# Second input's four transfers issued together, and its row squares moved to the first attention half

## The chip, the cores and the metric

The kernel runs on one core of one Trainium2 chip. The metric is the device time of one execution in microseconds (us); less is better. A core has a matmul engine (TensorE, PE in the profile; PEld is its weight load), a vector engine (VectorE, DVE), a scalar engine (ScalarE, ACT), GpSimd (POOL) and an engine that here only issues transfers (SyncE, SP). Each engine works through its own instructions in the order in which the program gives them. Transfers between the chip's main memory (HBM) and on-chip memory (SBUF) run on 16 DMA engines.

## The reference

```python
for layer in range(DEPTH):                      # DEPTH = 1, x is (1, 256, 2048)
    h = rms_norm(x, ln_pre_g[layer])
    proj = jnp.einsum('bsd,de->bse', h, w_in[layer])
    rnn_x, rnn_gate, q, k, v, attn_gate, g_rnn, g_attn = split_columns(proj)
    hr = rg_lru(rnn_x, ...)                     # convolution, gates, linear recurrence over tokens
    y_rnn = jnp.einsum('bsc,cd->bsd', hr * jax.nn.silu(rnn_gate), w_rnn_out[layer])
    ...                                         # q, k rotated; 24 heads in 3 groups with their own dilation
    y_attn = jnp.einsum('bsc,cd->bsd', o * jax.nn.silu(attn_gate), w_attn_out[layer])
    merged = jax.nn.sigmoid(g_rnn) * y_rnn + jax.nn.sigmoid(g_attn) * y_attn
    y = jnp.einsum('bsd,de->bse', merged, w_o[layer])
    x = x + rms_norm(y, ln_post_g[layer])
```

`rms_norm` divides each token's row by the root of its mean square. The kernel multiplies by the gain before the projections and by the row's factor (`rstd`) after them.

## The kernel before

Every projection is made with float32 split in two: a high half (`wh`, `xh`) and a low half (`wl`, `xl`), and three matmuls (lines 283 to 285) in place of one: wh x xh, wl x xh, wh x xl. A projection of 512 columns has 16 rows of weight tiles. It goes in eight steps of a *pair* of them; with two token halves a pair is 12 matmuls. The weights come as transfers of 1 MB (`raw_...`, two pairs each, line 230) into three buffers, and each pair is split by ACT into `wh` (line 256) and by DVE into `wl` (line 257), into four buffers. `next_pair` keeps the splits some three pairs ahead of PE. The weight pairs of projection ga0 are called ga_0, ga_2, ... ga_14 here, by the first of their two tile rows.

The input is needed twice: for attention with its tokens in a turned order (`xh`, `xl`), and in their natural order for the gates and the recurrent branch. The second one comes in four transfers of 512 KB (`xnr0` to `xnr3`, line 179) and is split with the gain into `nh` by ACT (line 151) and `nl` by DVE (line 152), two instructions at a time. Its row factors `rstd_t` come from `row_stats` (lines 307 to 321): four transfers of rows (`xst`), four ACT squares that also add up, then a square root and a reciprocal.

The order of the program is: projections q, k (three groups), v (three groups) and the attention gate (`ag`) of half 0 of the heads, the same for half 1, then four gates `ga0` to `ga3` on the second x, and then the recurrent branch, its output and the last projection. Between the steps of a projection, `tick` lets other work proceed: the scores of a head, the shipping of its turned probabilities (`pt4` to `pt7` in half 1: 16 transfers of 32 KB each, line 84), their copy into `pr` (line 555), the weighted sums (`oo`, line 569). `load_in_time` is a generator that is advanced once per step of `ag1` and then of the gates (`along` in `proj_tok`). What it and the other jobs emit falls into the engines' queues at that place. SP's queue holds all transfers. A transfer into a tile waits until the last reader of the buffer's former tile is done; a raw buffer's last reader is the DVE split. Tiles of 512 KB share a pool of 29 buffers.

Of the kernel before, what the change touches and what calls it, by code (L numbers as in the profile page):

```python
# [42 lines left out]
def hybrid_block(ctx: ExitStack, tc: tile.TileContext, xc_rows, xct, xn_rows, xnt, par, g_post, w_in, w_rg, w_ig,  # L43
# [15 lines left out]
    def bigt(name, dt=F32):  # L59
        return big.tile([P, 1024], dt, name=name, tag="big", bufs=NBIG)  # L60
# [25 lines left out]
    def split_turned(t, name):  # L86

        h, l = bigt(f"{name}h", F32R), bigt(f"{name}l", F32R)
        src, h4, l4 = (a.rearrange(f"p ({o}) -> p u c i", u=8, c=4, i=32)
                       for a, o in ((t, "u c i"), (h, "c u i"), (l, "c u i")))  # L90
        nc.scalar.activation(h4, src, AF.Copy)
        nc.vector.tensor_tensor(l4, src, h4.bitcast(F32), op=ALU.subtract)
        return h, l
# [16 lines left out]
    def tick():  # L110
        now[0] += 1
        heavy = True
        for job in list(jobs):
            if job[0] <= now[0] and (heavy or job[2]):
                heavy = heavy and job[2]
                step(job)

    def step(job):
        try:
            d = next(job[1])  # L120
            job[2] = isinstance(d, float)
            job[0] = now[0] + int(d)
        except StopIteration:
            jobs.remove(job)

    def spawn(gen):
        job = [now[0], gen, False]
        jobs.append(job)
        step(job)
# [17 lines left out]
    def split_x(t, h, l, q, k):  # L147

        s = slice(k * S, (k + 1) * S)
        gk = par_sb[:, GP, q * 4 + k:q * 4 + k + 1]  # L150
        nc.scalar.activation(h[:, s], t[:, s], AF.Copy, scale=gk)
        nc.vector.scalar_tensor_tensor(l[:, s], t[:, s], gk, h[:, s].bitcast(F32), op0=ALU.mult, op1=ALU.subtract)
# [20 lines left out]

    def load_in_time():

        ts = [bigt(f"xnr{q}") for q in range(2)]

        def fetch(q):
            nc.sync.dma_start(ts[q].rearrange("p (k n) -> p k n", n=S),
                              xnt[q * 512:(q + 1) * 512, :].rearrange("(k p) n -> p k n", p=P))  # L180

        fetch(0)
        yield
        fetch(1)
        yield
        for q in range(4):
            h, l = bigt(f"nh{q}", F32R), bigt(f"nl{q}", F32R)
            if q >= 2:
                ts.append(bigt(f"xnr{q}"))
                fetch(q)  # L190
            for k in range(4):
                split_x(ts[q], h, l, q, k)
                nh.append(h[:, k * S:(k + 1) * S])
                nl.append(l[:, k * S:(k + 1) * S])
                if k % 2:
                    yield
# [73 lines left out]
    def next_pair(tag):  # L270
        while len(ready) <= AHEAD:
            p = next(stream, None)
            if p is None:
                break
            ready.append(p)
        p = ready.pop(0)
        assert p[0] == tag
        return p[1], p[2]

    def mm_tok(acc, t, k, lh, ll, wh, wl, nk):  # L280
        ts = slice(t * P, (t + 1) * P)
        acc = acc[t] if isinstance(acc, list) else acc[:, t, :]
        nc.tensor.matmul(acc, lh[k][:, ts], wh, start=(k == 0), stop=False)  # L283
        nc.tensor.matmul(acc, lh[k][:, ts], wl, start=False, stop=False)  # L284
        nc.tensor.matmul(acc, ll[k][:, ts], wh, start=False, stop=(k == nk - 1))  # L285

    def proj_tok(lh, ll, nk, tag, acc=None, steps=None, along=iter(())):

        if acc is None:
            acc = ps_acc.tile([P, 2, GRP], F32, name=f"acc_{tag}", tag="acc")  # L290
        for _ in range(steps or nk // 2):
            k0, pair = next_pair(tag)
            for kk, (wh, wl) in enumerate(pair):
                for t in range(2):
                    mm_tok(acc, t, k0 + kk, lh, ll, wh, wl, nk)
            next(along, None)
            tick()
        return acc
# [6 lines left out]
    rstd_t = const.tile([P, 2], F32, name="rstd_t")  # L305

    def row_stats(dst, rows, name):
        ss = const.tile([P, 2, 2], F32, name=f"ss{name}")
        xs = [[bigt(f"xs{name}{t}{i}") for i in range(2)] for t in range(2)]
        for t in range(2):  # L310
            for i in range(2):
                nc.sync.dma_start(xs[t][i], rows[t * P:(t + 1) * P, i * 1024:(i + 1) * 1024])
        yield 2
        for t in range(2):
            for i in range(2):
                nc.scalar.activation(xs[t][i], xs[t][i], AF.Square, accum_out=ss[:, t, i:i + 1])
                yield 1
        nc.vector.tensor_reduce(dst, ss, axis=AX.X, op=ALU.add)
        nc.vector.tensor_scalar(dst, dst, 1.0 / D, EPS, op0=ALU.mult, op1=ALU.add)
        nc.scalar.activation(dst, dst, AF.Sqrt)  # L320
        nc.vector.reciprocal(dst, dst)

    def norm_stats(kind, acc):
        yield from row_stats(rstd, xc_rows, "c")
        yield from qk_group(kind, 0, 0, acc)
# [138 lines left out]
    def qk_group(kind, g, half, acc):  # L464
        tr = bigt(f"{kind}T{g}{half}")
        hf = ROT // 2
        turned = Turn(tr, f"{kind}{g}{half}")
        for t in range(2):
            if t:
                yield 1  # L470
            r = work.tile([P, 4, 4, 32], F32, name=f"{kind}r{g}{half}{t}", tag="rope")
            nc.scalar.activation(r.rearrange("p e h j -> p h e j"), acc[:, t, :].rearrange("p (h e j) -> p h e j", h=4, e=4),
                                 AF.Copy, scale=rstd[:, t:t + 1])
            m = work.tile([P, 2, 4, ROT], F32, name=f"{kind}m{g}{half}{t}", tag="ropem")
            rot = r[:, 0]
            cosb = trig_sb[:, t, 0, :].unsqueeze(1).to_broadcast([P, 4, ROT])
            nc.vector.tensor_tensor(m[:, 0], rot, cosb, op=ALU.mult)
            for o in range(2):
                sn = trig_sb[:, t, 1, o * hf:(o + 1) * hf].unsqueeze(1).to_broadcast([P, 4, hf])
                nc.vector.tensor_tensor(m[:, 1, :, o * hf:(o + 1) * hf], rot[:, :, (1 - o) * hf:(2 - o) * hf], sn,  # L480
                                        op=ALU.mult)
            nc.vector.tensor_tensor(rot, m[:, 0], m[:, 1], op=ALU.add)
            turned.take(t, r.rearrange("p e h j -> p (e h j)"))
        yield from turned.ship()
        yield 5
        if g == 0:
            qkv[kind, g, half] = tuple(a.rearrange("p (c n) -> p c n", c=4) for a in split_turned(tr, f"{kind}s{half}"))
        elif kind == "q":
            q = bigt(f"qc{g}{half}")
            nc.scalar.activation(q.rearrange("p (h u i) -> p u h i", h=4, u=8), tr.rearrange("p (u h i) -> p u h i", u=8, h=4), AF.Copy)  # L490
            qkv[kind, g, half] = q.rearrange("p (h n) -> p h n", h=4)
        else:
            qkv[kind, g, half] = tr.rearrange("p (t b h i) -> p t b h i", t=2, b=4, h=4)
# [95 lines left out]
    def after(n, gen):  # L589
        yield n  # L590
        yield from gen


    for half in range(2):
        for g in range(NG):
            if half == 0 and g == 0:
                spawn(norm_stats("q", proj_tok(xh, xl, NK, "q00")))
                nc.sync.dma_start(trig_sb, trig)
                nc.sync.dma_start(mask_sb, masks)
                spawn(qk_group("k", g, half, proj_tok(xh, xl, NK, "k00")))  # L600
            else:
                spawn(qk_group("q", g, half, proj_tok(xh, xl, NK, f"q{g}{half}")))
                spawn(qk_group("k", g, half, proj_tok(xh, xl, NK, f"k{g}{half}")))
        for hh in range(4):
            spawn(after(3, scores(half, hh)))
        if half:
            spawn(row_stats(rstd_t, xn_rows, "t"))
        for g in range(NG):
            v_group(g, half, proj_tok(xh, xl, NK, f"v{g}{half}"))
        x2 = load_in_time() if half else iter(())  # L610
        attn_gate(half, proj_tok(xh, xl, NK, f"ag{half}", along=x2))
        for hh in range(4):
            spawn(after(2, weighted(half, hh)))
# [183 lines left out]
```

## Time and profile before

| what | value |
|---|---|
| median of 3 runs | 1080.38 us (1079.28 to 1081.52) |
| the profiled execution: its time | 1080.39 us |
| its span, from the first to the last instruction | 1078.6 us |
| PE busy | 1054.8 us (98%) |
| DVE busy | 652.9 us (61%) |
| ACT busy | 581.0 us (54%) |
| mean granted clock | 0.991 |

The busy shares are means over the span. PE is near 100% almost everywhere, and the page's row of 40 slices shows PE at 9 tenths or more in all but four of them: the first (8), the last (6), and two next to each other from 458 to 512 us (7 and 8), where the granted clock also falls to 8 tenths. "Granted clock" 1.00 is 2.4 GHz, 0.50 is 1.2 GHz. In a timeline the first number is the start in us from the span's start, the second the length, and the brackets give the idle time of the engine before it and what ended that. A matmul of PE is shown with 0.39 us, but one starts each 0.23 us, since they overlap.

### The profile page before, as it was taken

Reading aid. Unit: us, or ns where it says so; the run is one execution under the profiler, and the core shown is the slowest. Engines: PE = TensorE matmul, PEld = TensorE weight load, DVE = VectorE, ACT = ScalarE, POOL = GpSimd, SP = SyncE. Lnnn points to the kernel's source line nnn. Section 1 sums busy time; section 2 is a strip of 40 time slices with the busy share of each in tenths; the row PEclk is TensorE's granted clock in tenths of the full one; section 3 lists DMA queues with packets and bytes.
Section 4 is the critical chain, followed back from the end, with each engine's and each line's share of the span. In section 5 each row is a group of like instructions: output and inputs, shape, how many; then the busy total and the mean of one; then the engine's idle time right before and its main releaser. Section 6 shows DMA issues by size and latency. Waiting matters only on the chain.

```text
span 1078.6 us, 12939 instructions
## 1 busy us (share of the span) xinstructions
PE 1054.8 (98%) x4774; PEld 875.0 (81%) x4774; DVE 652.9 (61%) x831; ACT 581.0 (54%) x716; POOL 3.0 (0%) x7
## 2 busy tenths in 40 slices
PE   8999999999999999978999999999999999999996
PEld 7888888888888888857888888888888888888785
DVE  6666555646655646445654585876757746666455
ACT  7645445553544545463644457657767665444443
POOL 0000000000000000000000000000000000000000
PEclk9999999999999999988999999999999999999999
DMA  9868675565767774744666665666666655666872
GB/s 325 313 199 266 209 230 170 160 221 193 233 204 244 249 252 156 230 154 148 205 201 212 213 215 192 203 227 200 206 199 213 217 170 199 197 209 204 288 255 78
DMA packets 153263, 228.03 MB, mean 211 GB/s; under 512 B 12528, under 2 KB 56304, under 8 KB 153200
## 3 DMA queue, kind: packets, MB, share of 16 engines
q1 hardware_dynamic: 153200, 227.21, 64.9%
q8 instruction: 37, 0.61, 0.2%
q14 instruction: 26, 0.21, 0.1%
HBM read 207.23 MB, written 2.10 MB: 194 GB/s over the span
## 4 chain that ended last, share of the span: by engine, by line
PE 46%; DVE 3%; DMA 2%; ACT 1%; SPq 1%; issue 0%; ACTq 0%; DVEq 0%
PE acc_rx L283 3%; PE acc_rx L284 3%; PE acc_rx L285 3%; PE acc_rg L285 3%; PE acc_rg L283 3%; PE acc_rg L284 3%; PE acc_gr L284 3%; PE acc_gr L285 3%; PE acc_gr L283 3%; PE acc_ga L284 2%; PE acc_ga L285 2%; PE acc_ga L283 2%; PE acc_o L284 2%; PE acc_o L285 2%; PE acc_o L283 2%; PE acc_ro L284 2%
## 5 line engine op out<-in xcount | busy, mean ns | idle before, releaser
L257 DVE TENSOR_TENSOR wl_v<-raw_v,wh_v 128x1024 fp32r<-128x1024 f32 x48 | 58.2, 1216 | 56.5 <-ACT wh_v L256 56.5
L257 DVE TENSOR_TENSOR wl_k<-raw_k,wh_k 128x1024 fp32r<-128x1024 f32 x48 | 58.2, 1217 | 44.7 <-ACT wh_k L256 44.7
L256 ACT ACTIVATE wh_k<-raw_k 128x1024 fp32r<-128x1024 f32 x48 | 50.7, 1059 | 60.7 <-PE acc_q L285 26.6
L257 DVE TENSOR_TENSOR wl_q<-raw_q,wh_q 128x1024 fp32r<-128x1024 f32 (+1 forms) x50 | 58.6, 1173 | 38.3 <-ACT wh_q L256 36.5
L283 PE MATMUL acc_v<-wh_v,xh 128*128 128x512 f32 x192 | 76.3, 398 | 0.0
L283 PE MATMUL acc_q<-wh_q,xh 128*128 128x512 f32 x192 | 75.3, 392 | 1.0 <-ACT wh_q L256 1.0
L284 PE MATMUL acc_q<-wl_q,xh 128*128 128x512 f32 x192 | 74.9, 390 | 0.8 <-DVE wl_q L257 0.8
L285 PE MATMUL acc_v<-wh_v,xl 128*128 128x512 f32 x192 | 74.9, 390 | 0.0
L285 PE MATMUL acc_q<-wh_q,xl 128*128 128x512 f32 x192 | 74.9, 390 | 0.0
L284 PE MATMUL acc_v<-wl_v,xh 128*128 128x512 f32 x192 | 74.7, 389 | 0.0
L284 PE MATMUL acc_k<-wl_k,xh 128*128 128x512 f32 x192 | 74.7, 389 | 0.0
L283 PE MATMUL acc_k<-wh_k,xh 128*128 128x512 f32 x192 | 74.7, 389 | 0.0
L285 PE MATMUL acc_k<-wh_k,xl 128*128 128x512 f32 x192 | 74.7, 389 | 0.0
L256 ACT ACTIVATE wh_q<-raw_q 128x1024 fp32r<-128x1024 f32 (+1 forms) x50 | 51.0, 1025 | 42.7 <-PE acc_q L285 22.2
L256 ACT ACTIVATE wh_v<-raw_v 128x1024 fp32r<-128x1024 f32 x48 | 50.2, 1054 | 33.3 <-PE acc_v L285 23.4
L283 PE MATMUL acc_ga<-wh_ga,nh 128*128 128x512 f32 x128 | 52.0, 406 | 8.0 <-ACT wh_ga L256 8.0
L257 DVE TENSOR_TENSOR wl_rx<-raw_rx,wh_rx 128x1024 fp32r<-128x1024 f32 x32 | 39.1, 1223 | 34.0 <-ACT wh_rx L256 33.8
L257 DVE TENSOR_TENSOR wl_ga<-raw_ga,wh_ga 128x1024 fp32r<-128x1024 f32 x32 | 39.2, 1224 | 30.5 <-ACT wh_ga L256 30.4
L256 ACT ACTIVATE wh_ro<-raw_ro 128x1024 fp32r<-128x1024 f32 x32 | 33.5, 1058 | 38.3 <-PE acc_ro L285 33.6
L257 DVE TENSOR_TENSOR wl_rg<-raw_rg,wh_rg 128x1024 fp32r<-128x1024 f32 x32 | 38.8, 1220 | 25.4 <-ACT wh_rg L256 25.4
L284 PE MATMUL acc_ga<-wl_ga,nh 128*128 128x512 f32 x128 | 52.2, 408 | 1.7 <-DVE wl_ga L257 1.7
L257 DVE TENSOR_TENSOR wl_o<-raw_o,wh_o 128x1024 fp32r<-128x1024 f32 x32 | 38.3, 1220 | 24.2 <-ACT wh_o L256 24.2
(301 smaller groups left out, 2681.5 us busy)
## 6 DMA issues: line engine op xcount, KB each, us to landing
raw_k<-in_w_in_dram SPq DMA_DIRECT2D x24, 1024.0 KB, 5.4
raw_v<-in_w_in_dram SPq DMA_DIRECT2D x24, 1024.0 KB, 5.4
raw_q<-in_w_in_dram SPq DMA_DIRECT2D x20, 1024.0 KB, 5.7
raw_ga<-in_w_in_dram SPq DMA_DIRECT2D x16, 1024.0 KB, 5.2
raw_rx<-in_w_in_dram SPq DMA_DIRECT2D x16, 1024.0 KB, 5.5
raw_rg<-in_w_in_dram SPq DMA_DIRECT2D x16, 1024.0 KB, 5.1
raw_gr<-in_w_in_dram SPq DMA_DIRECT2D x16, 1024.0 KB, 5.5
raw_ro<-in_w_rnn_out_dram SPq DMA_DIRECT2D x16, 1024.0 KB, 5.4
```

The costliest lines, as they stand in the source:

```text
L256: nc.scalar.activation(h[:, i:i + m, :], src, AF.Copy)
L257: nc.vector.tensor_tensor(l[:, i:i + m, :], src, h[:, i:i + m, :].bitcast(F32), op=ALU.subtract)
L283: nc.tensor.matmul(acc, lh[k][:, ts], wh, start=(k == 0), stop=False)
L284: nc.tensor.matmul(acc, lh[k][:, ts], wl, start=False, stop=False)
L285: nc.tensor.matmul(acc, ll[k][:, ts], wh, start=False, stop=(k == nk - 1))
```

## The change

All four transfers of the second x are issued at two neighbouring steps of `ag1` (two and two), and the splits of its pairs begin one step later than before. `row_stats` for the second norm is started in half 0, after the projections of group 1, and no longer in half 1.

```diff
--- before.py
+++ after.py
@@ -173,21 +173,16 @@
 
     def load_in_time():
 
-        ts = [bigt(f"xnr{q}") for q in range(2)]
-
-        def fetch(q):
+        ts = []
+        for q in range(4):
+            ts.append(bigt(f"xnr{q}"))
             nc.sync.dma_start(ts[q].rearrange("p (k n) -> p k n", n=S),
                               xnt[q * 512:(q + 1) * 512, :].rearrange("(k p) n -> p k n", p=P))
-
-        fetch(0)
-        yield
-        fetch(1)
+            if q % 2:
+                yield
         yield
         for q in range(4):
             h, l = bigt(f"nh{q}", F32R), bigt(f"nl{q}", F32R)
-            if q >= 2:
-                ts.append(bigt(f"xnr{q}"))
-                fetch(q)
             for k in range(4):
                 split_x(ts[q], h, l, q, k)
                 nh.append(h[:, k * S:(k + 1) * S])
@@ -601,10 +596,10 @@
             else:
                 spawn(qk_group("q", g, half, proj_tok(xh, xl, NK, f"q{g}{half}")))
                 spawn(qk_group("k", g, half, proj_tok(xh, xl, NK, f"k{g}{half}")))
+            if half == 0 and g == 1:
+                spawn(row_stats(rstd_t, xn_rows, "t"))
         for hh in range(4):
             spawn(after(3, scores(half, hh)))
-        if half:
-            spawn(row_stats(rstd_t, xn_rows, "t"))
         for g in range(NG):
             v_group(g, half, proj_tok(xh, xl, NK, f"v{g}{half}"))
         x2 = load_in_time() if half else iter(())
```

The order in SP's queue at the end of half 1 was this (raw_ga0_0 is the first 1 MB of weights of ga0, pt7 the last head's turned probabilities, xnr0 to xnr3 the second x):

```order
L230 DMA raw_ga0_0_3704<-in_w_in_dram 128x4x512
L179 DMA xnr0_3718<-in_xnt_dram 128x4x256
L84 DMA pt7_3692<-trp7_3693 32x2x128 x4
L179 DMA xnr1_3719<-in_xnt_dram 128x4x256
L84 DMA pt7_3692<-trp7_3693 32x2x128 x4
L230 DMA raw_ga0_1_3754<-in_w_in_dram 128x4x512
L84 DMA pt7_3692<-trp7_3693 32x2x128 x8
L230 DMA raw_ga0_2_3808<-in_w_in_dram 128x4x512
L230 DMA raw_ga0_3_3857<-in_w_in_dram 128x4x512
L179 DMA xnr2_3873<-in_xnt_dram 128x4x256
L230 DMA raw_ga1_0_3914<-in_w_in_dram 128x4x512
L179 DMA xnr3_3930<-in_xnt_dram 128x4x256
```

It is now this:

```order
L225 DMA raw_ga0_0_3712<-in_w_in_dram 128x4x512
L179 DMA xnr0_3726<-in_xnt_dram 128x4x256
L179 DMA xnr1_3728<-in_xnt_dram 128x4x256
L84 DMA pt7_3700<-trp7_3701 32x2x128 x4
L179 DMA xnr2_3750<-in_xnt_dram 128x4x256
L179 DMA xnr3_3752<-in_xnt_dram 128x4x256
L84 DMA pt7_3700<-trp7_3701 32x2x128 x4
L225 DMA raw_ga0_1_3765<-in_w_in_dram 128x4x512
L84 DMA pt7_3700<-trp7_3701 32x2x128 x8
L225 DMA raw_ga0_2_3813<-in_w_in_dram 128x4x512
```

xnr2 and xnr3 moved from behind three weight transfers to between the pt7 transfers.

On ACT, from the split of pair ag1_12 to that of ga0_4, there stood (xst are the squares, nh the split of the second x, pr7 the copy of the last head's probabilities):

```order
L256 ACTIVATE wh_ag1_12_3779<-raw_ag1_3_3654 128x1024
L151 ACTIVATE nh0_3768<-xnr0_3718,par_sb_94 128x256 x2
L316 ACTIVATE xst10_3081,sst_3078<-xst10_3081 128x1024
L256 ACTIVATE wh_ag1_14_3804<-raw_ag1_3_3654 128x1024
L151 ACTIVATE nh1_3822<-xnr1_3719,par_sb_94 128x256 x2
L316 ACTIVATE xst11_3082,sst_3078<-xst11_3082 128x1024
L256 ACTIVATE wh_ga0_0_3829<-raw_ga0_0_3704 128x1024
...
L256 ACTIVATE wh_ga0_2_3853<-raw_ga0_0_3704 128x1024
L151 ACTIVATE nh2_3871<-xnr2_3873,par_sb_94 128x256 x2
L555 ACTIVATE pr7_3879<-pt7_3692 128x4x4x32 x2
L256 ACTIVATE wh_ga0_4_3882<-raw_ga0_1_3754 128x1024
```

There now stands:

```order
L251 ACTIVATE wh_ag1_12_3783<-raw_ag1_3_3662 128x1024
L151 ACTIVATE nh0_3799<-xnr0_3726,par_sb_94 128x256 x2
L251 ACTIVATE wh_ag1_14_3809<-raw_ag1_3_3662 128x1024
L151 ACTIVATE nh0_3799<-xnr0_3726,par_sb_94 128x256 x2
L251 ACTIVATE wh_ga0_0_3831<-raw_ga0_0_3712 128x1024
L151 ACTIVATE nh1_3847<-xnr1_3728,par_sb_94 128x256 x2
L251 ACTIVATE wh_ga0_2_3853<-raw_ga0_0_3712 128x1024
L151 ACTIVATE nh1_3847<-xnr1_3728,par_sb_94 128x256 x2
L550 ACTIVATE pr7_3875<-pt7_3700 128x4x4x32 x2
L251 ACTIVATE wh_ga0_4_3878<-raw_ga0_1_3765 128x1024
```

The squares and the square root are gone from here, and only nh0 and nh1, no longer nh2, stand ahead of pr7. In the first half the squares stand on ACT between the weight splits of group 2's q and k (q20, k20), and their transfers on SP behind the last q20 transfer:

```order
L225 DMA raw_q20_3_832<-in_w_in_dram 128x4x512
L307 DMA xst00_873<-in_xn_rows_dram 128x1024
L307 DMA xst01_874<-in_xn_rows_dram 128x1024
L307 DMA xst10_875<-in_xn_rows_dram 128x1024
L307 DMA xst11_876<-in_xn_rows_dram 128x1024
L225 DMA raw_k20_0_886<-in_w_in_dram 128x4x512
```

Before, the two weight transfers stood there next to each other. PE's order is the same in both kernels.

## Rows read from the trace of the kernel before

**Rows 1.** PE's waits between 430 and 530: total us, times, longest us.
```profile
PE acc_ga L283 <- ACT wh_ga L256: 8.0, 2, 4.9
PE acc_ga L284 <- DVE wl_ga L257: 1.7, 3, 0.8
```

**Rows 2.** Stretches: length, busy PE, PEld, DVE, ACT, POOL; PEclk, DMA share, GB/s.
```profile
460.00:465.00 5.00, 3.57 (x14) 2.66 (x15) 3.59 (x6) 5.00 (x9) 0.00 (x0) 1.00 0.79 256
...
480.00:485.00 5.00, 4.05 (x9) 2.87 (x10) 2.04 (x4) 4.98 (x9) 0.00 (x0) 0.50 0.00 0
```

**Rows 3.** Timeline of SP's DMA queue: start, length, what is issued.
```profile
450.22 0.53 SPq L230 DMA_DIRECT2D raw_ga<-in_w_in_dram  x1
...
450.85 0.51 SPq L179 DMA_DIRECT2D xnr<-in_xnt_dram  x1
...
451.42 3.17 SPq L84 DMA_DIRECT2D pt<-trp  x4
...
459.60 5.64 SPq L84 DMA_DIRECT2D pt<-trp  x8
...
471.41 0.50 SPq L179 DMA_DIRECT2D xnr<-in_xnt_dram  x1
...
487.79 0.50 SPq L179 DMA_DIRECT2D xnr<-in_xnt_dram  x1
```

**Rows 4.** Timeline of ACT; in brackets the idle time before, and its releaser.
```profile
457.71 0.91 ACT L151 ACTIVATE nh<-xnr,par_sb 128x256 fp32r<-128x256 f32 x2 [1.89 <-DMA xnr<-in_xnt_dram]
...
477.54 0.91 ACT L151 ACTIVATE nh<-xnr,par_sb 128x256 fp32r<-128x256 f32 x2 [7.84 <-DMA xnr<-in_xnt_dram]
...
478.35 1.13 ACT L555 ACTIVATE pr<-pt 128x512 f32<-128x512 f32 x2
```

**Rows 5.** Timeline of PE in the same stretch.
```profile
459.57 0.40 PE L285 MATMUL acc_ag<-wh_ag,xl 128*128 128x512 f32 x1
...
480.49 0.79 PE L283 MATMUL acc_ga<-wh_ga,nh 128*128 128x512 f32 x1 [4.86 <-ACT wh_ga L256]
...
481.75 0.79 PE L284 MATMUL acc_ga<-wl_ga,nh 128*128 128x512 f32 x1 [0.47 <-DVE wl_ga L257]
...
486.45 1.95 PE L569 MATMUL oo<-v,pr 128*128 128x128 f32 x16
...
488.16 0.48 PE L283 MATMUL acc_ga<-wh_ga,nh 128*128 128x512 f32 x1
...
491.00 1.95 PE L569 MATMUL oo<-v,pr 128*128 128x128 f32 x16
...
504.44 0.48 PE L283 MATMUL acc_ga<-wh_ga,nh 128*128 128x512 f32 x1
```

**Rows 6.** Timeline of DVE in the same stretch.
```profile
486.12 1.22 DVE L257 TENSOR_TENSOR wl_ga<-raw_ga,wh_ga 128x1024 fp32r<-128x1024 f32 x1
```

**Rows 7.** DMA issues from 450.7, then from 465.2: KB each, us to landing.
```profile
raw_ga<-in_w_in_dram SPq DMA_DIRECT2D x1, 1024.0 KB, 5.7
xnr<-in_xnt_dram SPq DMA_DIRECT2D x1, 512.0 KB, 6.8
...
pt<-trp SPq DMA_DIRECT2D x1, 32.0 KB, 2.3
```

**Rows 8.** A stretch near the kernel's start, columns as in rows 2.
```profile
10.00:15.00 5.00, 3.27 (x13) 2.11 (x12) 3.51 (x7) 3.87 (x8) 0.00 (x0) 1.00 1.06 381
```

**Rows 9.** First half: timelines of SP and ACT, then the tile xst.
```profile
93.67 0.54 SPq L230 DMA_DIRECT2D raw_q<-in_w_in_dram  x1
...
106.38 1.06 ACT L256 ACTIVATE wh_q<-raw_q 128x1024 fp32r<-128x1024 f32 x1 [1.66 <-PE acc_q L285]
...
L316 ACT ACTIVATE xst<-xst x4: 1041/1046/1051, 445.6 to 464.1; 128x1024 f32<-128x1024 f32 x4
L316 ACT ACTIVATION_READ_ACCUMULATOR xst<-xst x4: 185/186/193, 446.6 to 465.0; 128x1 f32 x4
...
DMA to landing us min/median/max: 6.6/7.7/8.7
```


## Prediction

> **What bounds the kernel now.** I read the page first: TensorE (PE) is busy for almost the whole span, so time can only be won where PE waits, where its clock is low, or at the two ends. The list of PE's waits around the second x shows that the waiting has one place: the first gate projection on the second x, acc_ga, waited 8.0 us in two waits for the high halves of its weights (wh_ga, made on ACT) and 1.7 us in three for the low halves (wl_ga, made on DVE) [rows 1]. The stretches of 5 us say the same from the other side: 3.57 us of 5 busy from 460, and from 480 to 485 the granted clock is 0.50, the lower of the two levels, 1.2 GHz [rows 2]. The reader is to see that the clock is still 1.00 where PE idles from 460, and low only behind a longer wait, that of 4.9.
>
> Why are wh_ga late? ACT runs in order, and just before those weights it stood for 1.89 us until xnr landed, and again for 7.84 us [rows 4]. xnr is the second x. The queue of SP explains it: its first transfer goes out at 450.85, but the third only at 471.41 and the fourth at 487.79 [rows 3]. They stand behind weight transfers (raw_ga) that wait for a buffer, and such a buffer comes free only when DVE has split older weights, which needs ACT. So ACT waits for xnr, xnr for SP, SP for a raw buffer, and the raw buffer for PE, ACT and DVE. The stall feeds itself twice.
>
> How much is it worth? PE's last undisturbed matmul before all this starts at 459.57, and pair ga_10 (the sixth of the eight weight pairs of ga0) begins at 504.44 [rows 5]. With a pitch of 0.23 the next matmul was due at 459.80, so the stretch is 44.64 us long. The work in it is four pairs of twelve matmuls at 2.72 (where PE sets the pace, ACT splits one pair in 1.06 and waits 1.66 for PE [rows 9]), four groups oo at 1.71 (486.45 to 488.16), and three pairs that follow an oo at 2.84 (488.16 to 491.00) [rows 5]: 10.88 + 6.84 + 8.52 = 26.2 us. The loss is 44.6 - 26.2 = **18.4 us**, waits and low clock together. That is the most that the change can give back here.
>
> **The change, part by part.** (1) The four xnr transfers are issued at two neighbouring steps, all ahead of the second raw_ga transfer. By SP's rhythm xnr0 and xnr1 go out at about 450.9 and 451.4, xnr2 and xnr3 after four pt transfers, at about 455.3 and 455.9. The buffers of xnr2 and xnr3 were last read by half 1's score phase (pt4 and qs1h), ahead of ag1 on their engines, so I see no new wait for a buffer. Both ACT waits for xnr go away.
>
> (2) The squares leave this stretch: four ACTIVATEs of about 1.05 us with a read of 0.19 each [rows 9], a square root with its table load, and three tiny DVE instructions. ACT then reaches the split of ag_14 earlier. Replayed by the rows: nh0 cannot start before xnr0 lands at 457.71 [rows 4], 0.91 for two nh, then the split of ag_14 by about 459.7 and its low half on DVE 1.2 later, 460.9. PE needs it at 459.80 + 2.72 = 462.5. So the waits before and in ag_12 go, and ga_0 starts at 465.2.
>
> (3) What is late next? ACT has split pair ga_2 and the nh behind it by about 464.5 (three nh couples and two splits from 459.7) and then stands before pr7 (the copy of the last head's turned probabilities), which waits for all sixteen pt7 transfers. Before, this copy started at 478.35, behind xnr2 [rows 4], and the wait was covered. Behind it on ACT stand wh_ga_4, nh2, the attention gate (agz, ags) with its table load, and wh_ga_6. PE will wait for those. So the time T at which pr7 starts decides the sum.
>
> T from rows: the last pt7 transfer was issued at 459.60 + 5.64 = 465.24 and landed 2.3 us later, at 467.5 [rows 3, 7]. Two more issues now stand ahead of it, 0.57 each (450.85 to 451.42): T is at least 467.5 + 1.1 = 468.6. From above: their bytes share the 16 DMA engines too. raw_ga, issued at 450.22, landed at 455.9 and xnr0, right behind it, at 450.85 + 6.8 = 457.65 [rows 3, 7], so 512 KB cost 1.73 us, two of them 3.5; if none of it fits into a gap, T = 468.6 + 3.5 = 472.1. I take the middle, **T = 470.3**, because the DMA engines still had some room then (0.79 busy from 460) [rows 2].
>
> The Trainium skill, page "DMA: Bandwidth & Descriptors", section Specifications, gives a core about 358 GB/s from HBM; by that 512 KB would be an estimated 1.46 us, the two 2.9, and T in the middle 470.0 in place of 470.3. No row shows that rate for an xnr alone; the sum keeps the row's 1.73.
>
> (4) From T on I carry over the distances of before, where the same ACT instructions stood in the same order behind pr7: wl_ga_4's matmul started at 481.75, which is 478.35 + 3.4; wl_ga_6 was split at 486.12 to 487.34, which is 9.0 behind 478.35 [rows 4 to 6]. PE comes to ga_4 at 465.2 + 2 x 2.72 + 1.71 = 472.4 and could take its low half at 472.7, but gets it at T + 3.4 = 473.7: a wait of 1.0. The rest of the pair takes 2.5, oo5 1.7; the low half of ga_6 comes at T + 9.0 = 479.3 where PE was ready at T + 7.9: 1.1 more. Then 2.5, oo6 1.7, ga_8 2.84 and oo7 1.71: ga_10 begins at T + 17.8 = 488.1. Before it was 504.44, so the gain is 486.7 - T, or **16.4 us**, with a cap of 18.4 (reached at T below 468.3). The bounds of T give 18.1 and 14.6.
>
> (5) Does the clock stay up? Two waits of about 1 us in some 7 us. At the start of the kernel PE was busy 3.27 us of 5, 1.7 idle, with the clock at 1.00 [rows 8]; it fell behind the wait of 4.9 [rows 1, 2]. The expected waits are close to the first, so I count no low clock.
>
> (6) What is added in the first half: four xst transfers of 512 KB right behind raw_q at 93.67, four squares and the square root. Landing took 6.6 to 8.7 us [rows 9], so they are there from about 101 to 105; the squares stand behind four splits, the third of which started at 106.38, one each 2.72. ACT's free time there is 1.66 us in each 2.72 [rows 9], and a square with its read is 1.24: it fits. I cost this part at nothing. Its cover is that ACT waits for PE, not PE for ACT; if a square waits for its transfer, ACT must be held for more than about two pairs of PE, 5 us (of four buffers for split weights at least two are full), before PE feels it, and without any cover the four cost 5.0 us. SP's next weight transfer waits for a raw buffer, one of which comes free every second pair, 5.4 us, so four issues at SP's pace of 0.6 ahead of it, 2.4 us, delay nothing. The square root no longer needs a table of its own where it now stands, between copies; the removed load lay in ACT time that had slack, so it is not counted.
>
> **Sum.** Profiled execution 1080.39 us (span 1078.6 and 1.8 around it; the median of the runs is 1080.38, the same), less 16.4: **1064.0 us**. Behind ga0 the page's slices show PE at nine tenths or more, so the rest should move as a block.
>
> **The rivals.** *Full cover*: pt7 isn't delayed by the extra transfers, or lands in gaps; T below 468.3, gain 18.4, 1062.0 us. For it: the last pt7 had landed at 467.5. Against: two issues and 1 MB stand in front of it. *The wait moves to pt7 and takes the clock with it*: transfers of pt7 queue behind xnr1 to xnr3 longer than their bytes say, because each issue on SP can also wait for an earlier one to land; T near 474.5, so PE waits 5 us at ga_4 and the clock falls once more. Gain 486.7 - 474.5 = 12.2, less the 2.2 that a pair took longer at the lower level (4.70 from 481.75 to 486.45 for what takes 2.5): 10.0, so 1070.4 us. For it: four pt issues behind xnr0 took 3.17 us, 0.8 each, those behind raw_ga 0.7 [rows 3], so SP does feel what is in flight. Against: only two of the four are new ahead of pt7. *Slower than before*: the xst transfers in the first half hold ACT, and through it the weights of k20. It decides from the point at which ACT stands for more than 5 + 16.4 = 21.4 us before a square; a landing of 31 us (a stand of 23) would cost about 2 us net, 1082. The longest landing seen was 8.7 us [rows 9]. *The change does nothing*: the tile buffers of xnr2 and xnr3 come free only with ga0, so their transfers wait where they are now and hold SP's queue: 1080. The order of last readers speaks against it.
>
> **How the numbers follow.** The likeliest case (T from 468.3 to 472.1) 0.72, full cover 0.10, the wait at pt7 with a lower clock 0.14, no effect 0.02, slower 0.02. A measurement of this kernel can tell about 0.2% (2 us) from no change. Faster: 0.72 + 0.10 + 0.14 = 0.96. The range: from 1061.5 (full cover, and half a microsecond of spread between runs) up to 1068.0, which is the likeliest case's upper end, 1080.4 - 14.6 = 1065.8, plus one short fall of the clock; it leaves out most of the pt7 rival and the last two, under 0.2.
>
> **What would show each step right or wrong.** Right: four xnr issues before 457, no ACT wait for xnr above 2 us after the first, a new ACT wait of about 6 us for pt in front of pr7, PE waits of acc_ga of 1 us or less each on wl_ga, granted clock 1.00 from 460 to 510, and ga_10 near 488. Step 3 is wrong if pr7 starts outside 468 to 472.5; step 5 if a stretch there shows a clock below 0.95; step 6 if PE shows a wait between 95 and 130 or ACT waits more than 2 us for xst. The sum is wrong if a wait that the long stall has hidden so far, for instance weights of ga1 behind the same queue, comes up after ga0.

## The result and the profile after

The changed kernel took 1065.12 us (median of 4 runs, 1064.78 to 1066.12), the kernel before 1080.52 in the same comparison (median of 4, 1079.28 to 1081.52): ratio 0.986, 95% interval 0.9843 to 0.9877. The prediction was 1064.0, with a range of 1061.5 to 1068.0. The profiled execution of the changed kernel took 1065.36 us (span 1063.6, mean granted clock 0.998 in place of 0.991).

First the queue of SP after the change, which answers to [rows 3]. (Lines 151 and 179 have stayed, those from 230 on are 5 less than before, 6 less in the kernels with the earlier fetch.)

```profile
450.95 1.14 SPq L179 DMA_DIRECT2D xnr<-in_xnt_dram  x2
452.82 2.54 SPq L84 DMA_DIRECT2D pt<-trp  x4
455.41 1.71 SPq L179 DMA_DIRECT2D xnr<-in_xnt_dram  x2
458.21 3.73 SPq L84 DMA_DIRECT2D pt<-trp  x4
...
462.62 5.68 SPq L84 DMA_DIRECT2D pt<-trp  x8
```

All four transfers of the second x are out by 457.1; before, the fourth went out at 487.79. Next ACT's timeline, which answers to [rows 4]:

```profile
458.22 0.91 ACT L151 ACTIVATE nh<-xnr,par_sb 128x256 fp32r<-128x256 f32 x2 [1.40 <-DMA xnr<-in_xnt_dram]
...
470.22 1.15 ACT L550 ACTIVATE pr<-pt 128x512 f32<-128x512 f32 x2 [5.85 <-DMA pt<-trp]
```

The wait of 7.84 for xnr is gone, and a wait of 5.85 for pt, the last head's turned probabilities, stands in front of `pr7`. Behind it, at 471.28, comes the split wh_ga_4. A third wait of ACT for the second x, which [rows 4] does not show, is gone too; in the kernel before it was this, behind the fourth transfer:

```profile
494.17 0.91 ACT L151 ACTIVATE nh<-xnr,par_sb 128x256 fp32r<-128x256 f32 x2 [8.28 <-DMA xnr<-in_xnt_dram]
```

PE's timeline, for [rows 5], with the first matmuls of the second attention gate, of ga0 and of the recurrent branch (`acc_rx`), so that the stretch can be measured:

```profile
443.63 0.39 PE L278 MATMUL acc_ag<-wh_ag,xh 128*128 128x512 f32 x1
...
465.39 0.39 PE L278 MATMUL acc_ga<-wh_ga,nh 128*128 128x512 f32 x1
...
473.63 0.50 PE L279 MATMUL acc_ga<-wl_ga,nh 128*128 128x512 f32 x1 [0.62 <-DVE wl_ga L252]
...
479.28 0.50 PE L279 MATMUL acc_ga<-wl_ga,nh 128*128 128x512 f32 x1 [0.84 <-DVE wl_ga L252]
...
488.10 0.48 PE L278 MATMUL acc_ga<-wh_ga,nh 128*128 128x512 f32 x1
...
561.64 0.39 PE L278 MATMUL acc_rx<-wh_rx,nh 128*128 128x512 f32 x1
```

ga_10 begins at 488.10, and at 504.44 before. PE's waits from 430 to 530 have shrunk from the 9.7 us of [rows 1], and 1.5 more for weights of the attention gate that are not shown there, to one line:

```profile
PE acc_ga L279 <- DVE wl_ga L252: 1.5, 2, 0.8
```

And the stretches, columns as in [rows 2]: from 440 to 505 no stretch is below a clock of 1.00, and PE's idle time is small and lies from 470 to 480.

```profile
470.00:475.00 5.00, 4.38 (x28) 3.69 (x27) 2.02 (x3) 4.76 (x8) 0.00 (x0) 1.00 0.97 366
475.00:480.00 5.00, 4.16 (x27) 3.53 (x26) 3.13 (x5) 5.00 (x9) 0.00 (x0) 1.00 0.12 45
```

### The profile page after: what moved, and what is told of

It reads as the page before. It is cut to its first block, busy times and chain, and to the rows that moved or that the text cites. A ratio compares the mean times of both kernels' runs of the same rounds, so it can differ in the third digit from the quotient of the medians.

```text
span 1063.6 us, 12933 instructions
## 1 busy us (share of the span) xinstructions
PE 1049.1 (99%) x4774; PEld 871.5 (82%) x4774; DVE 652.2 (61%) x831; ACT 579.6 (54%) x715; POOL 3.0 (0%) x7
## 4 chain that ended last, share of the span: by engine, by line
PE 79%; DMA 7%; DVE 5%; SPq 4%; ACT 3%; issue 1%; ACTq 0%; DVEq 0%
PE acc_k L279 4%; PE acc_k L278 4%; PE acc_k L280 4%; PE acc_q L279 4%; PE acc_q L280 4%; PE acc_q L278 4%; PE acc_v L278 3%; PE acc_v L280 3%; PE acc_v L279 3%; PE acc_rx L278 3%; PE acc_rx L279 3%; PE acc_rg L278 3%; PE acc_rg L280 3%; PE acc_rx L280 3%; PE acc_rg L279 3%; SPq L84 3%
## 5 line engine op out<-in xcount | busy, mean ns | idle before, releaser
L252 DVE TENSOR_TENSOR wl_gr<-raw_gr,wh_gr 128x1024 fp32r<-128x1024 f32 x32 | 38.7, 1216 | 23.0 <-ACT wh_gr L251 22.8
L252 DVE TENSOR_TENSOR wl_ro<-raw_ro,wh_ro 128x1024 fp32r<-128x1024 f32 x32 | 38.4, 1216 | 21.9 <-ACT wh_ro L251 21.8
```

Source lines behind the costliest of these rows:

```text
L252: nc.vector.tensor_tensor(l[:, i:i + m, :], src, h[:, i:i + m, :].bitcast(F32), op=ALU.subtract)
```

## The experiments

Each kernel was timed beside the kernel before on the same chip. Chips differ (the median of before was 1080.5 beside the first result, then 1080.1, 1077.9, 1078.9 and 1078.8 us), so ratios are compared between chips, and microseconds on one. This table has, for one profiled execution of each, the time between the first matmuls named above, and the last projection (o) from its first to its last matmul. For the changed kernel it is 465.39 - 443.63 = 21.76 and 561.64 - 465.39 = 96.25.

| kernel | ratio to before (95%) | ag1 to ga0 | ga0 to rx | sum | o |
|---|---|---|---|---|---|
| before | | 24.06 | 110.66 | 134.72 | 87.89 |
| before, again (e10) | | 22.82 | 109.84 | 132.66 | 87.67 |
| changed | 0.986 (0.9843 to 0.9877) | 21.76 | 96.25 | 118.01 | 89.20 |
| changed, again (e6) | 0.9848 (0.9830 to 0.9866) | 21.76 | 94.24 | 116.00 | 87.68 |
| four transfers together, alone (e1) | 0.9852 (0.9838 to 0.9866) | 21.76 | 94.98 | 116.74 | 88.66 |
| the same, again (e7) | 0.9851 (0.9832 to 0.9869) | 21.76 | 94.50 | 116.26 | 88.02 |
| squares moved alone (e2) | 0.9995 (0.9985 to 1.0005) | 22.50 | 107.66 | 130.16 | 88.39 |
| the same, again (e8) | 0.9988 (0.9976 to 1.0000) | 21.94 | 108.05 | 129.99 | 88.12 |
| the same, third (e11) | | 22.07 | 108.75 | 130.82 | 90.60 |
| changed, fetched earlier (e3) | 0.9846 (0.9826 to 0.9866) | 21.79 | 94.24 | 116.03 | 88.14 |
| changed, `pr7` one step later (e4) | 0.9849 (0.9836 to 0.9863) | 21.93 | 94.24 | 116.17 | 88.84 |
| fetched earlier, squares left (e9) | 0.9959 (0.9943 to 0.9974) | 33.41 | 94.24 | 127.65 | 87.81 |
| e9 without the squares' instructions (e12) | 0.9855 (0.9838 to 0.9871) | 21.76 | 94.24 | 116.00 | 88.92 |
| e3 with 26 tile buffers (e13) | 0.9915 (0.9898 to 0.9933) | 24.11 | 94.24 | 118.35 | 88.91 |

**e1, e7: the four transfers together, the squares left where they were.**
```diff
@@ against the changed kernel
-            if half == 0 and g == 1:
-                spawn(row_stats(rstd_t, xn_rows, "t"))
...
+        if half:
+            spawn(row_stats(rstd_t, xn_rows, "t"))
```


> The four transfers together, the squares left in half 1. Theory (the copy pr7 waits for pt7 and sets the pace, so ACT time saved ahead of it is lost again): ACT still reaches pr7 before pt7 has landed, at about 468.5, pr7 starts near 470.2 as in the changed kernel, PE loses up to 0.7 us at ga_2 and wins it back at ga_4, pair ga_10 begins at 488.1 to 488.4, and the time is that of the changed kernel, 1065.1 within 0.5 us. Rival (the squares are worth what ga_0 gained, 1.9 us): 1067.0.

Measured: 1063.81 us (1063.28 to 1065.78). ACT was busy with squares and splits until 468.3 and then waited only 1.22 for pt, where the changed kernel waited 5.85; `pr7` started at 469.52. So the squares' time is inside that wait, as the theory had it. The time was 1.3 under the expected 1065.1; how far the changed kernel itself moves is seen below (e6).

> The four transfers issued together, the row squares left in the second half, once more, so that it stands beside the changed kernel on one chip. Theory (the squares' move is worth nothing once the four transfers are together, because the wait for the last head's transposed probabilities takes up what it frees): the two medians within 0.7 of each other, ACT again at that wait, shorter than the changed kernel's 5.9 (about 1.2) and ended at the same time (469.5 to 470.3). Rival (the move itself costs, in the first half): this one lower by 1.0 to 1.5.

Measured: 1062.10 us (1061.23 to 1062.82), the changed kernel beside it (e6) 1061.72 (1061.12 to 1062.46): 0.4 apart. `pr7` at 468.82 behind a wait of 1.38, 0.7 earlier than expected. The theory holds: with the four transfers together, the move of the squares is worth nothing that shows.

In e1 and e7 the splits of the second x still begin one step later than before, as in the changed kernel. No run took that apart from the order of the issues. By the program it cannot have brought xnr2 and xnr3 forward: before, their issue stood among those splits, and a later start alone would have put it later.

**e2, e8, e11: the squares moved alone, the transfers as before.**
```diff
@@ against the kernel before
+            if half == 0 and g == 1:
+                spawn(row_stats(rstd_t, xn_rows, "t"))
...
-        if half:
-            spawn(row_stats(rstd_t, xn_rows, "t"))
```


> The squares moved to half 0, the transfers of the second x as before. Theory (the transfers hang on the splits through the raw buffers, so ACT's earlier start is passed on once, not lost): xnr2 is issued near 466.8 in place of 471.4 and lands near 473, xnr3 near 483, both long waits of ACT for xnr stay, the clock falls again, and ga_10 begins near 499.8 where it was 504.4: 4.7 us faster than before, 1075.8. Rival (only the 1.9 us of ga_0 are won, the rest is set by the transfers): 1078.5. If the two parts add up, this one and e1 together give the gain of 15.4; by the theory they give about 20.

Measured: 1079.13 us (12 runs, 1078.02 to 1081.95), 1 us under before by the medians, and the interval of the ratio takes in no change at all (the theory's 4.7 us would be 0.9956): neither number was met, the rival's 1078.5 was nearer. In the profiled execution ACT waits for the second x more than before, since it now has nothing else to do:

```profile
476.36 0.91 ACT L151 ACTIVATE nh<-xnr,par_sb 128x256 fp32r<-128x256 f32 x2 [10.18 <-DMA xnr<-in_xnt_dram]
```

Yet the stretch from ag1 to rx is 4.6 shorter than in the first execution of before. The other executions were made to find out which of the two is typical.

> The squares moved alone, once more: the first profiled execution lost 1.7 us in the first 20 us to a low stretch of the clock (matmuls 0.43 us apart in place of 0.23) and won 4.6 in the second projections, as the theory's 4.7 had it, yet the median of 12 runs was only 1 us under that of before. Theory (gain of 4.6 there in each execution, and the early low stretch is chance): no low stretch in the first 20 us, median 1075.8 to 1077. Rival (the third and fourth transfer land as it happens, and the stall moves with them): median 1078.5 to 1079.5, and in this execution the second projections gain 0 to 3.

Measured: 1076.76 us (12 runs, 1073.77 to 1078.47) beside 1077.89 for before: again 1.1 by the medians and, in the profiled execution, 4.7 in the stretch. The median was the theory's (1075.8 to 1077), and the stretch too, but before was lower on this chip as well, so the ratio gained next to nothing. The profiled executions of e2 and e8 were 1.0 and 1.8 us under the medians of their kernels, so both lie at the fast end of their runs.

> The kernel of before, a second profiled execution. Between the start of the attention gate of the second half and that of the first projection behind the gates, the first one took 134.7 us (443.26 to 577.98); the two executions with the squares moved alone took 130.2 and 130.0. Theory (4.6 us is what the moved squares win there): 134.7 again, within 0.7. Rival (that span changes from one execution to the next with the landing of the third and fourth transfer and with the clock): another value, 130.5 to 133.5.

> The squares moved alone, a third profiled execution, beside a second one of before on the same chip. Theory: 130.0 to 130.3 from the second half's attention gate to the first projection behind the gates, 4.6 under before's. Rival (the median, 1 us lower, is all that the move wins): 131 to 134, within 2 of before's.

Measured: 132.66 for before (theory 134.7; the rival's "it changes" is right), 130.82 with the squares moved: 1.8 under before, as the rival had it (within 2), and just below its 131. So the stretch of before moves by 2 us from one execution to the next, and the move alone wins 1.8 to 4.7 of it. That is more than the 1.0 and 1.1 us of the medians; where the rest goes is not settled. Two of the three executions with the squares moved had a low clock near the start (below), but so had executions of other kernels.

**e3: all four transfers issued in the value projections of half 1**, some 80 us earlier.
```diff
@@ against the changed kernel
-            if q % 2:
-                yield
-        yield
+        for _ in range(4):
+            yield
...
         for hh in range(4):
             spawn(after(3, scores(half, hh)))
+        x2 = load_in_time() if half else iter(())
+        next(x2, None)
...
-        x2 = load_in_time() if half else iter(())
         attn_gate(half, proj_tok(xh, xl, NK, f"ag{half}", along=x2))
```


> As the changed kernel, but all four transfers of the second x are issued where the squares' transfers stood before, in the v projections of half 1, and pt7 has SP's queue to itself and the weights. Theory (the extra issues and bytes ahead of pt7 delay pr7, and that costs PE 2.0 us at ga_4 and ga_6): pr7 starts near 465.6, no PE wait from 460 to 490, ga_10 near 486.1, 1063.1. Rival (the wait for pt7 is hidden or another transfer takes its place): 1065.1. A loss, if the transfers now hold up the v weights: PE waits between 370 and 400, above 1066.

**e4: the copy `pr7` one step later**, so that wh_ga_4 stands ahead of it on ACT.
```diff
@@ against the changed kernel
-        yield 3
+        yield 4 if h == 7 else 3
         prob[h] = bigt(f"pr{h}").rearrange("p (t c n) -> p t c n", t=2, c=4)
```


> As the changed kernel, but the copy pr7 is put one step later, so on ACT it stands behind the split of ga_4 and a couple of nh. Theory (what costs is only what stands behind pr7 in ACT's order): pr7 still starts near 470.2, wh_ga_4 is made at 467.5 as its weights land, the gate's sigmoids start 1.7 us earlier, no wait or one below 0.3 us at ga_4 and ga_6, ga_10 near 486.1 to 486.4, 1063.2. Rival (ga_4 and ga_6 are set by their weights' landing, not by pr7): 1065.1.

Measured: e3 1063.01 us (1061.14 to 1067.03), e4 1063.99 (1062.86 to 1064.78), on the chip on which e1 had 1063.81. `pr7` started at 464.27 in e3 and at 469.72 in e4. In both profiled executions PE waits for nothing from 430 to 530, ga_10 begins at 485.48 and 486.50, and ga0 to rx takes 94.24, the least of all executions here: six of the kernels have just that. So what stands behind `pr7` on ACT was the last thing that PE waited for. But the ratios are those of the changed kernel run again. The 2 us that both were expected to win had been lost in the changed kernel's first profiled execution, and are not lost in each:

> The changed kernel once more, word for word. Its first profiled execution won 16.3 us between the start of the second projections and the stage behind them, and gave back 0.5 us at the first half's attention gate and 1.3 us in the last projection. Theory (those two are the chance of a transfer's landing, not the change): median 1065.1, within 0.7; the stage behind again starts with the same gain inside the second projections (16.3 to 16.9 relative to the first half), the two losses come out at other sizes (0.1 to 0.6, 0.2 to 1.5). Rival (the earlier squares and the shifted buffers cost them): 0.5 and 1.3 again, within 0.1.

Measured: 1061.72 us (1061.12 to 1062.46). `pr7` started at 467.24 (in brackets what ACT waited), and PE waited for nothing from 430 to 530; ga0 to rx is 94.24 without any further edit.

```profile
467.24 1.15 ACT L550 ACTIVATE pr<-pt 128x512 f32<-128x512 f32 x2 [5.57 <-DMA pt<-trp]
```

The median is under the expected 1065.1, but before was 2.6 lower on this chip as well. The stretch is 18.7 shorter than in the first execution of before and 16.7 shorter than in the second; the o stage took 87.68, as before, and the first gate 21.76 (22.68 before, 23.18 in the changed kernel's first execution). So the loss of 1.3 in o and that of 0.5 at the first gate did not come back, as the theory of chance has it, though the sizes it named (0.1 to 0.6 and 0.2 to 1.5) were not met.

**e9: the early fetch, with the squares left in half 1** (e3 with e1's edit).

> The four transfers issued in the value projections, and the squares left in the second half. Theory (the squares only fill the wait for the last head's probabilities): 1063.0, within 0.7, the same as with the squares moved; ACT reaches the copy of the last head's probabilities after they landed, at about 466.5 to 467.5, and TensorE waits for nothing from 430 to 530. Rival (4.7 us of squares come back on ACT's chain, since here that wait was only 1.9): 1065 to 1066, a TensorE wait of 1 to 2 for the weights of the first second projection.

Measured: 1073.78 us (1072.62 to 1074.60): both theories were far off. Between ag1 and ga0 TensorE loses 9.4 us against before and 11.6 against the kernels with the transfers together (33.41 for 21.76). It waits for weights of the gate, 4.1 us in two waits for wh_ag and 2.7 in four for wl_ag, and behind the longest wait the clock goes to 0.56 from 465 to 470:

```profile
465.76 0.79 PE L277 MATMUL acc_ag<-wh_ag,xh 128*128 128x512 f32 x1 [3.58 <-ACT wh_ag L250]
```

That split stands on ACT right behind a copy `pr` which waited for its pt, and the pt are late because ACT and SP stood still before. What they waited for is unexpected. These are the two copies on ACT, then the wait of SP's queue:

```profile
438.11 1.15 ACT L549 ACTIVATE pr<-pt 128x512 f32<-128x512 f32 x2 [6.62 <-PE ss L525]
...
463.62 1.15 ACT L549 ACTIVATE pr<-pt 128x512 f32<-128x512 f32 x2 [5.70 <-DMA pt<-trp]
```
```profile
SPq L84 <- PE ss L528: 12.0, 1, 12.0
```

SP's wait lies in the row of pt issues that begins at 424.13, and it ends at 438.10, like that of ACT.

Neither the copy `pr` nor the shipping of pt reads `ss`, the scores of a head. The first theory after it was that eight transfers at once make v's weights land late (a wait of ACT for raw_v of 6.5 us is in the trace), so e12 kept the transfers and left out the squares, with a constant in place of their sums:

```diff
@@ against e9, in row_stats
-                nc.scalar.activation(xs[t][i], xs[t][i], AF.Square, accum_out=ss[:, t, i:i + 1])
                 yield 1
+        nc.vector.memset(ss, 1024.0)
```


> The early fetch with the squares left in the second half, but their four ACT instructions taken out (the sums of squares are a constant in their place, so the second norms are not computed); their four transfers of 512 KB are still issued just ahead of the second x. In the kernel with the squares TensorE lost 9.4 us between the second attention gate and the projections behind it. Theory (the eight transfers together make the next weights land late, and the chain of the softmax slips by a step before any square has run): 7 to 9.4 of those are lost here too, time 0.995 to 0.997 of before's. Rival (the squares' time on ACT does it): at most 2 lost, time 0.985 to 0.987 of before's, as with the early fetch and the squares moved.

Measured: 1063.20 us (1062.87 to 1063.32); the rival's numbers, so the theory of the transfers falls (the same wait of 6.5 for raw_v is in e12, at no cost). But the rival's reason, the squares' time on ACT, doesn't hold either: in e9 the two long waits lie between 424 and 443, and the first square runs at 454.65. In e12 `pr4` starts at 430.96 and waits for nothing. What the squares do is to keep their four tiles of the shared pool of 29 from about 370 to 472; without them nothing reads these tiles once the transfers have landed. The theory then was that a tile which is needed takes over the buffer of one that a score matmul still reads: the last of those at L525 starts at 437.8 in e9, just before the waiting copy. e13 takes three buffers away from e3 and adds nothing:

```diff
-    NBIG = 29
+    NBIG = 26
```


> The early fetch with the squares in the first half, as it ran at 0.985 of before, and with 26 buffers in place of 29 in the ring of 128x1024 tiles; no transfer and no square is added. The kernel with the squares left in the second half held four more of those tiles from 370 to 472, and there the copy of the second half's first probabilities waited 6.6 us, to 438.1, for a score matmul, whose inputs' buffer it takes over. Theory (the price was buffers, not the squares' time on ACT): the same wait to 437 to 439, 29 to 34 us in place of 21.8 from the second attention gate to the second projections, and 0.994 to 0.999 of before's time. Rival (ACT's time): 21.8 there, and 0.984 to 0.987 of before's.

Measured: 1068.74 us (1068.37 to 1071.32). The wait is there, with no square and no added transfer:

```profile
436.52 1.15 ACT L549 ACTIVATE pr<-pt 128x512 f32<-128x512 f32 x2 [7.30 <-PE ss L525]
```

So too few buffers are enough to cause it. The last such score matmul starts at 436.2 here, and the copy again comes right behind it. But the time misses the theory: between ag1 and ga0 the price is only 2.3 us (24.11 for 21.79 in e3), not 7 to 12. Another 4.0 are lost far behind, since rx to o took 408.07 and 404.1 in the others. The large price of e9 goes with SP's 12.0, behind which the pt and the weights of the gate stand; e13 has 0.3 of that. That this wait too is for a buffer is suggested by its releaser and its end, but no run took it away alone.

## Why the prediction was right, step by step

- **Step 1 (four issues, no ACT wait for xnr):** forecast 450.9, 451.4, 455.3 and 455.9. The two couples went out at 450.95 and 455.41. "Both ACT waits for xnr go away" holds for the long one, and for the third of 8.28; of the first, 1.40 was left (1.89 before).
- **Step 2 (ga_0 at 465.2):** it came at 465.39. But the squares' leaving was not needed for it: in e1, where they stay, ag1 to ga0 is the same 21.76, and ACT does not wait for xnr at all. xnr0 goes out no earlier there (451.47), which points to the later start of the splits: it puts one more weight split ahead of the first nh. With the squares moved alone the stretch was 21.94 to 22.50. So either part nearly does it, and the step named one of them.
- **Step 3 (the wait moves to `pr7`, T = 470.3):** 470.22. The sum of the two delays was right and their parts were not: the last pt7 transfer was issued by 468.30, 3.1 later than before and not 1.1, and the copy began 1.9 behind that, so nothing of the 1.7 for shared bytes was left to add. The extra time lies in SP's queue: the four pt behind xnr1 took 2.54 and the four behind xnr3 3.73, and from 450 to 472 the queue has two waits, 2.3 us together, that the profile puts down to the landing of an xnr transfer (before: one of 1.1). That is the mechanism of the rival with the wait at pt7, at a small size. That T came out within 0.1 is luck: the parts made up for each other, and T moves by more than that from one execution to the next (below). From 450.9 to 457.2 the DMA engines moved 358 GB/s in the mean, pt's traffic included. The Trainium skill, page "DMA: Bandwidth & Descriptors", section Specifications, has the same 358 as the limit of a core for HBM. This case does not bear it out as a limit: from 10 to 25, where the transfers issued are loads from HBM, the changed kernel moved 376 GB/s, and [rows 8] has 381.
- **Step 4 (waits of 1.0 and 1.1, ga_10 at 488.1):** 0.62 and 0.84, and 488.10. The rule behind it, that PE loses what T exceeds ga_0's start by beyond 3.1 us (468.3 less 465.2), can be read against four executions in which ACT's order is that of the changed kernel:

| execution | T less start of ga_0 | less 3.1 | ga0 to rx above 94.24 |
|---|---|---|---|
| changed | 470.22 - 465.39 = 4.83 | 1.73 | 2.01 |
| e1 | 469.52 - 465.99 = 3.53 | 0.43 | 0.74 |
| e7 | 468.82 - 465.78 = 3.04 | none | 0.26 |
| e6 | 467.24 - 464.69 = 2.55 | none | 0.00 |

  It holds within some 0.3. What was too simple is that T is one number: it moves by 3 us between these executions, and "full cover" (given a chance of 0.10) is what e6 shows in the trace. By e6's ratio the changed kernel would take 0.9848 x 1080.4 = 1064.0, where the first comparison has 1065.1.
- **Step 5 (clock stays up):** 1.00 in each stretch from 440 to 505, as forecast. The working took the wait of 4.9 as the one behind which the clock fell. The trace of before has a second fall, behind a shorter wait, so the margin was smaller than it looked:

```profile
496.07 0.50 PE L283 MATMUL acc_ga<-wh_ga,nh 128*128 128x512 f32 x1 [3.13 <-ACT wh_ga L256]
```
```profile
495.00:500.00 5.00, 3.17 (x7) 2.33 (x8) 4.54 (x10) 4.66 (x7) 0.00 (x0) 0.65 0.00 0
```

- **Step 6 (the squares cost nothing in half 0):** no PE wait from 95 to 130, no wait of ACT for xst there (the squares run from 101.78 to 111), and e6 and e7 are 0.4 us apart. The square root runs at 114.31 without a table load, where before one of 1.28 us stood ahead of it.
- **The sum.** In the stretch it was 16.4 forecast, 134.72 - 118.01 = 16.7 measured. The time fell by 1080.39 - 1065.36 = 15.0. What did not hold is "the rest should move as a block": the changed execution lost 0.5 in the first half, at its gate, and 1.3 in the last projection. e6 shows neither, so by this one repeat they belong mostly to the execution and not to the change. A small cost in the last projection is not ruled out: over the nine executions with the four transfers together or earlier it took 88.5 on average (87.7 to 89.2), in the two of before 87.8. The cap of 18.4 comes out as 110.66 - 94.24 + 24.06 - 21.76 = 18.7 by the table.
- **The rivals.** No wait at pt7 took the clock down, and the xst transfers held nothing. "The change does nothing" rested on tile buffers; they were free here. With the fetch 80 us earlier, e9, whose squares hold four tiles for 100 us, is 12 us longer than e3 (0.9959 against 0.9846 of some 1079 us). So tile buffers may have been the rival with the most in it, at another place than the one that was named; e13 shows the wait from that cause, not the whole price.

What stays open: why the squares moved alone win 1.8 to 4.7 us in the stretch and 1 us in the median, what the order of the issues wins without the later start of the splits, and whether SP's wait of 12.0 alone makes e9's loss.

## What to carry to other kernels

When a transfer stands in a queue behind others that wait for the work it feeds, issue it ahead of them: the stall fed itself here, and nearly all of its 18 us came back when two issues moved ahead of three weight transfers (with the splits a step later). Before counting work taken from an engine as time won, look for the wait that stands behind it in the same queue: 5 us of squares were worth nothing in front of a wait of 6. And a tile held longer can cost time on engines that never touch it: where a releaser in the trace is an instruction whose result the waiting one doesn't read, look at the buffer.

## What the hardware showed that was not expected

The granted clock near the start differs between executions whose engines do nearly the same, and not by how long PE waited. In one execution (e2) PE was busy 3.36 us of the 5 from 10 to 15, its waits in them 0.89 and 0.75, and the clock fell. In another (e6, its row first) it was busy 3.02, with waits of 1.23 and 0.76, and the clock did not fall: it is 1.00 from 15 to 20 too. Nor did it fall at 3.27 in [rows 8]. Columns as there:

```profile
10.00:15.00 5.00, 3.02 (x13) 1.95 (x12) 3.26 (x7) 3.67 (x6) 0.00 (x0) 1.00 1.01 367
```
```profile
10.00:15.00 5.00, 3.36 (x13) 2.27 (x12) 3.00 (x6) 3.36 (x7) 0.00 (x0) 0.96 1.05 379
15.00:20.00 5.00, 5.00 (x17) 3.90 (x16) 4.74 (x7) 4.17 (x8) 0.00 (x0) 0.70 1.06 373
```

Four of the 14 profiled executions (e2, e7, e9, e11) had this; their first projection took 25.9 to 26.7 us in place of 23.9 to 24.9. So step 5's comparison with [rows 8] was weaker than it looked: that stretch keeps its clock in most executions and not in all.
